# A transformer block on one core: u and the merge's gates as half-size block products, the merge's two products moved apart

## Chip, core and metric

The kernel runs on one core of one Trainium2 chip. The metric is the device time of one execution in microseconds (us); lower is better. The chip's engines are named as the profile names them: PE (TensorE matmul), PEld (its weight loads), DVE (VectorE), ACT (ScalarE), POOL (GpSimd) and SP (SyncE, which here only issues DMAs).

## The reference, cut to what matters

All data is float32; 512 tokens, width 1024. `h` is a layer norm of the input. Eight slices of one wide projection of `h` feed two branches, which are merged through sigmoid gates:

```
proj = h @ w_in + b_in
u, v, q, f, i, g, ga, gb = split(proj)
y_a = gelu(u) * (per group of 128 channels: masked w_s @ layer_norm(gelu(v)) + b_s)
y_b = hgrn2(q, f, i) rms-normed * silu(g)
merged = sigmoid(ga) * (y_a @ w_a) + sigmoid(gb) * (y_b @ w_b)
h1  = layer_norm(ALPHA * h + merged @ w_o)
out = layer_norm(ALPHA * h1 + ffn(h1) + ple(h1, p))
```

## The kernel before, in words

Every float32 product is made of three matmuls on rounded parts: each operand is split into a high part (a copy rounded by ACT, line 63) and a low part (the difference, on DVE, line 66). `hh`, `hl` are the parts of `h` transposed (channels on partitions, 512 tokens along a row), `ybh`, `ybl` those of y_b, `yah`, `yal` those of y_a, `mgh`, `mgl` those of `merged`.

`gemm_a` (line 85) makes 256 output channels for all 512 tokens. It loads two weight units of 512 KB, splits each, and runs 48 matmuls with 512 columns. `gemm_b` and `mm_b` (lines 98 to 121) make the products whose result has tokens on partitions. `strassen` (line 165) makes the product of two 2x2 block matrices with seven block products in place of eight: X, Z, Y, Z2, Y2, W, Y3. Each block product is 24 matmuls with 256 columns (`product_a`, line 218). It needs sums of weight blocks: POOL adds t1 and t2 (line 185), and two more are accumulated by DMAs issued on POOL's queue (line 183). Its activation operands are blocks of the activations and sums of such blocks (`combine`, line 134). In the kernel before, only the feed-forward stage (`up`, line 897) uses it, eleven times; its weight tiles are in the pool `wx` (line 800) except for the first block and t1, which are in `wpool`.

The order of stages is: start, recurrence (f, q, g projections of four head pairs), v (line 699), then the part that the change touches:

- u by four `gemm_a` calls (`proj`, line 750), with `norm_v` (layer norm of v, line 711), `finish` of the last head pair (line 644, which gives the last part of y_b) and `mix` (line 732: the spatial product of v, then times gelu(u), then the split into `yah`, `yal`) in between;
- the merge (lines 781 to 795): four rounds of ga, w_a, gb, w_b, each a `gemm_a`, with the gates' sigmoid on ACT, two multiplies and an add on DVE, and the split into `mgh`, `mgl`; each round also calls `residual` (line 774), which loads a slice of x again and scales it on ACT and POOL into `r1`;
- w_o (line 809 on), first norm `norm1`, transposes `turn`, the gate of the embedding branch, then the feed-forward stage.

The order on each engine is set by the framework's scheduler: it walks the program by priority, which is program order, and issues on each engine the first instruction that its own timing model has as ready. So an independent later product can be pulled into a gap. On the chip each engine then runs its instructions in that fixed order and waits on semaphores. Tiles are taken from pools that are stacked on the left and on the right side of the on-chip memory; a pool opened after others were closed lies where those lay, and its tiles wait until the closed pools' tiles have been read for the last time. `wpool` has three buffers for raw weights and five for each split part; PSUM has four tiles of two banks.

Of the kernel before, what the change touches and what calls it, by code (L numbers as in the profile page):

```python
# [8 lines left out]
F32 = mybir.dt.float32  # L9
# [5 lines left out]
P = 128  # L15
D = 1024
# [17 lines left out]
def block_kernel(  # L34
# [50 lines left out]
    def gemm_a(ps, w, c0, acth, actl, name):  # L85

        for kh in range(2):
            h, l = unit_a(w, 4 * kh, c0, f"{name}_{kh}")
            for j in range(2):
                cs = slice(j * P, (j + 1) * P)  # L90
                for k in range(4):
                    kk = 4 * kh + k
                    first, last = kk == 0, kk == KT - 1
                    PE.matmul(ps[:, j, :], h[:, k, cs], acth[:, kk, :], start=first, stop=False)  # L94
                    PE.matmul(ps[:, j, :], h[:, k, cs], actl[:, kk, :], start=False, stop=False)  # L95
                    PE.matmul(ps[:, j, :], l[:, k, cs], acth[:, kk, :], start=False, stop=last)  # L96
# [602 lines left out]
    for c in range(2):  # L699
# [5 lines left out]
        for a in range(2):  # L705
# [15 lines left out]
    norm_v(3)  # L721
    hgb_cm.__exit__(None, None, None)

    rpool = ctx.enter_context(tc.tile_pool(name="rpool", bufs=1, side="right"))
    r1 = rpool.tile([P, TT, D], F32, name="r1")
    yapool_cm = tc.tile_pool(name="yapool", bufs=1, side="right")
    yapool = yapool_cm.__enter__()
    yah = yapool.tile([P, NH, T], F32R, name="yah")
    yal = yapool.tile([P, NH, T], F32R, name="yal")
    with tc.tile_pool(name="gm", bufs=1, side="right") as gp:  # L730
        bs = load_bc(gp, gm_b_s[0].rearrange("g t -> (g t)"), "bs")
        def mix(m, ug):
# [15 lines left out]
        prev = None  # L748
        for m in range(NH // 2):
            psu = proj(OU, m, "gu") if m else psu0  # L750
            ug = gp.tile([P, 2, T], F32, tag="ug", name=f"ug{m}", bufs=2)
            for a in range(2):
                S.activation(ug[:, a, :], psu[:, a, :], AF.Gelu_apprx_tanh, bias=bcol(OU, 2 * m + a))
            if m:
                mix(m - 1, prev)
            prev = ug
        mix(NH // 2 - 1, prev)
    gmv_cm.__exit__(None, None, None)


    mgpool_cm = tc.tile_pool(name="mgpool", bufs=1, side="right")
    mgpool = mgpool_cm.__enter__()
    mgh = mgpool.tile([P, KT, T], F32R, name="mgh")
    mgl = mgpool.tile([P, KT, T], F32R, name="mgl")
    with tc.tile_pool(name="mg", bufs=1) as mp:

        g0a = load_bc(mp, ln0_g, "g0a")
        b0a = load_bc(mp, ln0_b, "b0a")
        S.activation(g0a, g0a, AF.Copy, scale=ALPHA)
        S.activation(b0a, b0a, AF.Copy, scale=ALPHA)  # L770
        nmr = mp.tile([P, TT, 1], F32, name="nmr")
        V.scalar_tensor_tensor(out=nmr, in0=mr0[:, :, 0:1], scalar=-1.0, in1=mr0[:, :, 1:2], op0=ALU.mult, op1=ALU.mult)

        def residual(t):
            r = r1[:, t, :]
            nc.sync.dma_start(r, xv[:, t, :])
            S.activation(r, r, AF.Identity, scale=mr0[:, t, 1:2], bias=nmr[:, t, :])
            G.tensor_tensor(out=r, in0=r, in1=g0a, op=ALU.mult)
            G.tensor_tensor(out=r, in0=r, in1=b0a, op=ALU.add)

        for m in range(KT // 2):
            residual(m)
            res = []
            for nm, off, w, ah, al in (("a", OGA, wa, yah, yal), ("b", OGB, wb, ybh, ybl)):
                psg = ps_tile(f"ps_mg{nm}{m}")
                gemm_a(psg, win, off + 256 * m, hh, hl, f"g{nm}{m}")
                sg = mp.tile([P, 2, T], F32, tag="sg", name=f"sg{nm}{m}", bufs=3)
                for a in range(2):
                    S.activation(sg[:, a, :], psg[:, a, :], AF.Sigmoid, bias=bcol(off, 2 * m + a))
                psw = ps_tile(f"ps_mw{nm}{m}")  # L790
                gemm_a(psw, w, 256 * m, ah, al, f"w{nm}{m}")
                V.tensor_tensor(out=sg, in0=psw, in1=sg, op=ALU.mult)
                res.append(sg)
            V.tensor_tensor(out=res[0], in0=res[0], in1=res[1], op=ALU.add)
            split(mgh[:, 2 * m:2 * m + 2, :], mgl[:, 2 * m:2 * m + 2, :], res[0])
# [240 lines left out]
```

## Time and profile before

| what | value |
| --- | --- |
| median of 3 runs | 958.17 us (957.72 to 958.33) |
| the profiled execution's own time | 958.66 us |
| its span, first to last instruction | 956.9 us |
| PE busy | 936.7 us, 98% of the span |
| DVE, ACT, POOL busy | 592.0, 356.5, 218.2 us |
| mean granted clock of PE | 0.994 |

The profiled execution's time is its span and 1.8 us around it. PE's busy time is modelled (matmuls overlap in the pipeline), so the cost of a matmul is read from the distance of two starts, not from its length.

### The profile page before, as it was taken

Reading aid. Unit: us, or ns where it says so; the run is one execution under the profiler, and the core shown is the slowest. Engines: PE = TensorE matmul, PEld = TensorE weight load, DVE = VectorE, ACT = ScalarE, POOL = GpSimd, SP = SyncE. Lnnn points to the kernel's source line nnn. Section 1 sums busy time; section 2 is a strip of 40 time slices with the busy share of each in tenths; the row PEclk is TensorE's granted clock in tenths of the full one; section 3 lists DMA queues with packets and bytes.
Section 4 is the critical chain, followed back from the end, with each engine's and each line's share of the span. In section 5 each row is a group of like instructions: output and inputs, shape, how many; then the busy total and the mean of one; then the engine's idle time right before and its main releaser. Section 6 shows DMA issues by size and latency. Waiting matters only on the chain.

```text
span 956.9 us, 13354 instructions
## 1 busy us (share of the span) xinstructions
PE 936.7 (98%) x5545; PEld 811.5 (85%) x5545; DVE 592.0 (62%) x652; ACT 356.5 (37%) x424; POOL 218.2 (23%) x148
## 2 busy tenths in 40 slices
PE   6999999999999999999999999999999999999996
PEld 5788888878888888888888887899999999988885
DVE  6748753948348756323243278588878888557517
ACT  3343232332333463222232267454435445333211
POOL 6415230315005218000000000534433340000004
PEclk8999999999999999999999999999999999999999
DMA  7542223221522633322324313965676664258302
GB/s 255 176 143 89 68 66 110 67 78 57 174 88 67 204 104 110 104 94 88 110 88 156 126 50 99 248 181 133 168 165 176 154 153 113 77 189 269 124 25 88
DMA packets 85452, 120.46 MB, mean 126 GB/s; under 512 B 3992, under 2 KB 60944, under 8 KB 85392
## 3 DMA queue, kind: packets, MB, share of 16 engines
q1 hardware_dynamic: 80880, 105.92, 34.6%
q0 software_dynamic: 3168, 11.54, 7.1%
q10 hardware_dynamic: 1344, 2.16, 0.6%
q8 instruction: 43, 0.70, 0.3%
q14 instruction: 17, 0.14, 0.1%
HBM read 101.77 MB, written 6.29 MB: 113 GB/s over the span
## 4 chain that ended last, share of the span: by engine, by line
PE 87%; DVE 7%; ACT 2%; POOL 2%; issue 1%; DMA 1%; DVEq 0%; ACTq 0%; POOLq 0%
PE ps_f_b L226 4%; PE ps_f_b L228 4%; PE ps_f_b L229 4%; PE ps_d L102 4%; PE ps_d L100 4%; PE ps_d L101 4%; PE ps_f_a L226 3%; PE ps_f_a L229 3%; PE ps_f_a L228 3%; PE ps_mwa L95 2%; PE ps_mwa L96 2%; PE ps_mwa L94 2%; PE ps_i L102 2%; PE ps_f L94 2%; PE ps_v L100 2%; PE ps_mgb L95 2%
## 5 line engine op out<-in xcount | busy, mean ns | idle before, releaser
L253 POOL TENSOR_TENSOR mr<-mr,nhalf 128x1 f32<-128x1 f32 x12 | 8.2, 684 | 323.4 <-DVE mr L252 323.4
L63 ACT CAST wh_f<-raw_f 128x1024 fp32r<-128x1024 f32 x41 | 43.1, 1051 | 87.4 <-PE ps_f_b L228 38.4
L102 PE MATMUL ps_d<-wh_d,hidl 128*128 128x512 f32 x172 | 66.8, 389 | 0.0
L101 PE MATMUL ps_d<-wl_d,hidh 128*128 128x512 f32 x172 | 66.8, 389 | 0.0
L66 DVE TENSOR_TENSOR wl_f<-raw_f,wh_f 128x1024 fp32r<-128x1024 f32 x41 | 52.8, 1289 | 21.4 <-ACT wh_f L63 21.3
L100 PE MATMUL ps_d<-wh_d,hidh 128*128 128x512 f32 x172 | 66.0, 389 | 0.0
L66 DVE TENSOR_TENSOR wl_f_t<-t_f,wh_f_t 128x1024 fp32r<-128x1024 f32 x22 | 55.4, 2519 | 3.0 <-ACT wh_f_t L63 2.7
L185 POOL TENSOR_TENSOR t_f<-raw_f,raw_f 128x1024 f32<-128x1024 f32 x11 | 26.7, 2428 | 126.5 <-DVE wl_f L66 102.7
L63 ACT CAST wh_d<-raw_d 128x1024 fp32r<-128x1024 f32 x22 | 23.1, 1050 | 62.1 <-PE ps_d L102 23.3
L482 POOL TENSOR_TENSOR k<-sgm,lv 128x512 f32<-128x512 f32 x8 | 15.8, 1994 | 121.9 <-DVE lv L534 121.9
L66 DVE TENSOR_TENSOR wl_d<-raw_d,wh_d 128x1024 fp32r<-128x1024 f32 x22 | 26.9, 1223 | 18.8 <-ACT wh_d L63 18.8
L102 PEld LDWEIGHTS ps_d<-wh_d,hidl 128*128 128x128 f32 x172 | 32.3, 188 | 6.7
L101 PEld LDWEIGHTS ps_d<-wl_d,hidh 128*128 128x128 f32 x172 | 32.3, 188 | 6.6
L100 PEld LDWEIGHTS ps_d<-wh_d,hidh 128*128 128x128 f32 x172 | 32.2, 188 | 6.5
L63 ACT CAST wh_f_t<-t_f 128x1024 fp32r<-128x1024 f32 x22 | 23.2, 1053 | 32.5 <-PE ps_f_b L229 18.3
L185 POOL TENSOR_TENSOR t_f<-t_f,raw_f 128x1024 f32<-128x1024 f32 x11 | 35.1, 3189 | 0.9
L66 DVE TENSOR_TENSOR wl_wb<-raw_wb,wh_wb 128x1024 fp32r<-128x1024 f32 x8 | 14.2, 1778 | 25.7 <-ACT wh_wb L63 25.7
L66 DVE TENSOR_TENSOR wl_wa<-raw_wa,wh_wa 128x1024 fp32r<-128x1024 f32 x8 | 9.8, 1225 | 28.0 <-ACT wh_wa L63 28.0
L66 DVE TENSOR_TENSOR wl_wo<-raw_wo,wh_wo 128x1024 fp32r<-128x1024 f32 x8 | 9.8, 1223 | 25.8 <-ACT wh_wo L63 25.8
L102 PE MATMUL ps_i<-wh_i,hl 128*128 128x512 f32 x64 | 25.1, 391 | 0.4 <-DVE hl L66 0.4
L921 DVE TENSOR_TENSOR g<-p,ps_f_b 128x512 f32<-128x512 f32 x11 | 7.6, 688 | 28.8 <-PE ps_f_b L229 28.7
L94 PE MATMUL ps_q<-hh,wh_q 128*128 128x512 f32 x64 | 25.2, 394 | 0.0
(373 smaller groups left out, 3199.8 us busy)
## 6 DMA issues: line engine op xcount, KB each, us to landing
raw_f<-in_w_ffn_up_dram SPq DMA_DIRECT2D x22, 512.0 KB, 7.2
raw_f<-in_w_ffn_gate_dram SPq DMA_DIRECT2D x22, 512.0 KB, 3.8
raw_d<-in_w_ffn_down_dram SPq DMA_DIRECT2D x22, 512.0 KB, 3.6
raw_f<-raw_f POOLq DMA_DIRECT2D x11, 512.0 KB, 4.7
t_f<-raw_f POOLq DMA_DIRECT2D x11, 512.0 KB, 7.2
raw_i<-in_w_in_dram SPq DMA_DIRECT2D x8, 512.0 KB, 3.9
raw_f<-in_w_in_dram SPq DMA_DIRECT2D x8, 512.0 KB, 3.7
raw_q<-in_w_in_dram SPq DMA_DIRECT2D x8, 512.0 KB, 3.7
```

The costliest lines, as they stand in the source:

```text
L63: S.copy(h, src)
L66: (eng or V).tensor_tensor(out=l, in0=src, in1=h.bitcast(F32), op=ALU.subtract)
L94: PE.matmul(ps[:, j, :], h[:, k, cs], acth[:, kk, :], start=first, stop=False)
L95: PE.matmul(ps[:, j, :], h[:, k, cs], actl[:, kk, :], start=False, stop=False)
L96: PE.matmul(ps[:, j, :], l[:, k, cs], acth[:, kk, :], start=False, stop=last)
L100: PE.matmul(ps, acth[:, kk, ts], h[:, k, :], start=first, stop=False)
L101: PE.matmul(ps, acth[:, kk, ts], l[:, k, :], start=False, stop=False)
L102: PE.matmul(ps, actl[:, kk, ts], h[:, k, :], start=False, stop=last)
L185: G.tensor_tensor(out=d, in0=a, in1=b, op=ALU.add)
L226: PE.matmul(o, h[:, k, cs], ah[:, k, :], start=first and j == 0 and k == 0, stop=False, skip_group_check=True)
L228: PE.matmul(o, h[:, k, cs], al[:, k, :], start=False, stop=False, skip_group_check=True)
L229: PE.matmul(o, l[:, k, cs], ah[:, k, :], start=False, stop=last and j == 1 and k == 3, skip_group_check=True)
```

## The change

w_b's product runs right behind v, with its result kept in `mgf`. Meanwhile `combine_h` makes the sums of blocks of `h` that the block products need (POOL adds the parts up again, DVE subtracts, ACT and DVE split), and `mix` writes its result into `yaf` without u. u is then made by two calls of `group_a` (the body of `up`, made general), 512 channels each, and the gates by four calls, 256 channels of ga and of gb each. gelu(u) multiplies `yaf`; sigmoid(gb) multiplies `mgf`; sigmoid(ga) goes out to device memory and is loaded again for w_a's product, which comes last. `r1` takes the buffer of `mgf` and is formed during w_o. Pools: the weight tiles of the new groups (`wxh`) and their temporaries (`gt`) are opened on the left after `gmv` and `ybpool` are closed, so `wxh` lies where `ybh` and `ybl` lay; half of y_a's parts and the reloaded gate (`mg`) lie where `hh` and `hl` lay; the split of `merged` (now `mgs`, in a pool opened on the left during w_o) lies in part where the first half of y_a's parts lay.

```diff
     def gemm_a(ps, w, c0, acth, actl, name):
+        gemm_t(ps, w, c0, lambda kk: (acth[:, kk, :], actl[:, kk, :]), name)
+
+    def gemm_t(ps, w, c0, act, name):
...
-    def norm_v(t):
+    finish(M)
+    for t in range(TT):
         mr = gv.tile([P, 2], F32, tag="mrv", name=f"mrv{t}", bufs=2)
-        ln_stats(gv, [vn[:, t, 0:512], vn[:, t, 512:1024]], mr, f"v{t}")
+        ln_stats(gvv, [vn[:, t, 0:512], vn[:, t, 512:1024]], mr, f"v{t}")
         normed(vn[:, t, :], mr, gmg, gmb, True)
-
-    norm_v(0)
-    psu0 = proj(OU, 0, "gu")
-    norm_v(1)
-    finish(M)
-    norm_v(2)
-    norm_v(3)
...
+        def combine_h(i):
+            f = {}
+            for n, ks, t0 in (("21", 0, HT), ("22", 4, HT), ("11", 0, 0), ("12", 4, 0)):
+                at = (slice(None), slice(ks, ks + 4), slice(t0 + i * P, t0 + i * P + P))
+                f[n] = gp.tile([P, 4, P], F32, tag=f"f{n}", name=f"f{n}_{i}")
+                G.tensor_tensor(out=f[n], in0=hh[at].bitcast(F32), in1=hl[at].bitcast(F32), op=ALU.add)
+            f["s1"] = gp.tile([P, 4, P], F32, tag="fs1", name=f"fs1_{i}")
+            lo = slice(i * P, i * P + P)
+            for n, o, x, y in (("s1", "s1", "21", "22"), ("a7", "21", "21", "11"), ("a6", "11", "11", "s1"), ("a3", "12", "12", "11")):
+                V.tensor_tensor(out=f[o], in0=f[x], in1=f[y], op=ALU.subtract)
+                split(hcomb[n][0][:, :, lo], hcomb[n][1][:, :, lo], f[o])
...
-            V.tensor_tensor(out=mx, in0=mx, in1=ug, op=ALU.mult)
-            split(yah[:, 2 * m:2 * m + 2, :], yal[:, 2 * m:2 * m + 2, :], mx)
...
+        for m in range(KT // 2):
+            psw = ps_tile(f"ps_mwb{m}")
+            gemm_a(psw, wb, 256 * m, ybh, ybl, f"wb{m}")
+            S.copy(mgf[:, 2 * m:2 * m + 2, :], psw)
+            if m == 0:
+                combine_h(0)
+            elif m == 1:
+                mix(0)
+                mix(1)
+                combine_h(1)
+            elif m == 2:
+                mix(2)
+                mix(3)
     gmv_cm.__exit__(None, None, None)
+    ybpool_cm.__exit__(None, None, None)
...
+    def group_a(wx, fp, srcs, comb, name, out):
...
+        strassen(wx, [[src_a(w, 4 * a, c0) for w, c0 in srcs] for a in range(2)], name,
+                 "X Z Y Z2 Y2 W Y3", prod, evac)
...
+    with tc.tile_pool(name="wxh", bufs=1) as wx, tc.tile_pool(name="gt", bufs=1) as fp:
+        def out_u(q):
+            def out(i, j, o):
+                for a in range(2):
+                    S.activation(o[:, a, :], o[:, a, :], AF.Gelu_apprx_tanh, bias=bcol(OU, 4 * q + 2 * j + a))
+                y = yaf[:, 4 * q + 2 * j:4 * q + 2 * j + 2, HT * i:HT * i + HT]
+                V.tensor_tensor(out=y, in0=y, in1=o, op=ALU.mult)
...
+                if j == 0:
+                    S.dma_start(ga_dram[:, 2 * m:2 * m + 2, HT * i:HT * i + HT], o)
+                else:
+                    y = mgf[:, 2 * m:2 * m + 2, HT * i:HT * i + HT]
+                    V.tensor_tensor(out=y, in0=y, in1=o, op=ALU.mult)
...
+        for q in range(2):
+            group_a(wx, fp, [(win, OU + 512 * q + 256 * c) for c in range(2)], hcomb, f"u{q}", out_u(q))
+        yas_pool = yas_cm.__enter__()
+        for m in range(KT // 2):
+            group_a(wx, fp, [(win, OGA + 256 * m), (win, OGB + 256 * m)], hcomb, f"g{m}", out_g(m))
+            if m == 0:
+                split_ya(yas_pool, 0)
+    hpool_cm.__exit__(None, None, None)
...
+        split_ya(mp, 1)
+        for m in range(KT // 2):
+            ga = mp.tile([P, 2, T], F32, tag="ga", name=f"ga{m}", bufs=2)
+            nc.sync.dma_start(ga, ga_dram[:, 2 * m:2 * m + 2, :])
+            psw = ps_tile(f"ps_mwa{m}")
+            gemm_t(psw, wa, 256 * m, lambda kk: tuple(z[:, kk % 4, :] for z in yas[kk // 4]), f"wa{m}")
+            V.tensor_tensor(out=ga, in0=psw, in1=ga, op=ALU.mult)
+            o = mgf[:, 2 * m:2 * m + 2, :]
+            V.tensor_tensor(out=o, in0=o, in1=ga, op=ALU.add)
...
-        for m in range(KT // 2):
-            residual(m)
-            res = []
-            for nm, off, w, ah, al in (("a", OGA, wa, yah, yal), ("b", OGB, wb, ybh, ybl)):
-                psg = ps_tile(f"ps_mg{nm}{m}")
-                gemm_a(psg, win, off + 256 * m, hh, hl, f"g{nm}{m}")
...
```

## Rows read from the trace of the kernel before

**Rows 1.** The page's first part: busy us and share of each engine.

```profile
PE 936.7 (98%) x5545; PEld 811.5 (85%) x5545; DVE 592.0 (62%) x652; ACT 356.5 (37%) x424; POOL 218.2 (23%) x148
```

**Rows 2.** Waits of PE, longest first: total us, times, longest us.

```profile
PE ps_vec L379 <- DMA vec<-in_ln_b_dram: 7.2, 1, 7.2
```

**Rows 3.** Stretches: busy us of PE, PEld, DVE, ACT, POOL; clock; DMA.

```profile
295.00:347.00 52.00, 52.00 (x268) 44.36 (x266) 38.47 (x42) 22.54 (x26) 16.88 (x8) 1.00 0.43 137
...
605.00:815.00 210.00, 209.99 (x1770) 207.96 (x1769) 168.69 (x158) 98.89 (x111) 73.30 (x41) 1.00 0.66 160
```

**Rows 4.** Timeline of PE at the merge's products: start us, us, instruction.

```profile
434.76 0.39 PE L94 MATMUL ps_mga<-hh,wh_ga 128*128 128x512 f32 x1
...
445.64 0.39 PE L94 MATMUL ps_mwa<-yah,wh_wa 128*128 128x512 f32 x1
...
456.84 0.39 PE L94 MATMUL ps_mgb<-hh,wh_gb 128*128 128x512 f32 x1
...
511.38 0.39 PE L96 MATMUL ps_mgb<-hh,wl_gb 128*128 128x512 f32 x1
...
522.48 0.39 PE L100 MATMUL ps_wo<-wh_wo,mgh 128*128 128x512 f32 x1
```

**Rows 5.** Timeline of PE in the feed-forward stage: first matmuls of block products.

```profile
645.27 0.28 PE L226 MATMUL ps_f_b<-ca7h,wh_f_t 128*128 128x256 f32 x1
...
667.56 0.28 PE L229 MATMUL ps_f_a<-c11h,wl_f 128*128 128x256 f32 x1
...
670.19 0.28 PE L226 MATMUL ps_f_b<-c12h,wh_f 128*128 128x256 f32 x1
...
673.07 0.29 PE L226 MATMUL ps_f_b<-ca6h,wh_f_t 128*128 128x256 f32 x1
...
676.15 0.28 PE L226 MATMUL ps_f_b<-c22h,wh_f_t 128*128 128x256 f32 x1
...
678.87 0.28 PE L229 MATMUL ps_f_a<-cs1h,wl_f_t 128*128 128x256 f32 x1
...
801.37 0.28 PE L226 MATMUL ps_f_b<-ca7h,wh_f_t 128*128 128x256 f32 x1
```

**Rows 6.** Timeline of SP: issue of the first loads into the pool wx.

```profile
511.80 0.92 SPq L174 DMA_DIRECT2D raw_f<-in_w_ffn_up_dram  x2
```

**Rows 7.** The page's DMA issues: count, KB each, us from issue to landing.

```profile
raw_f<-in_w_ffn_up_dram SPq DMA_DIRECT2D x22, 512.0 KB, 7.2
raw_f<-in_w_ffn_gate_dram SPq DMA_DIRECT2D x22, 512.0 KB, 3.8
```

**Rows 8.** The page's costliest groups: busy us, mean ns | idle before, releaser.

```profile
L63 ACT CAST wh_f<-raw_f 128x1024 fp32r<-128x1024 f32 x41 | 43.1, 1051 | 87.4 <-PE ps_f_b L228 38.4
...
L66 DVE TENSOR_TENSOR wl_f<-raw_f,wh_f 128x1024 fp32r<-128x1024 f32 x41 | 52.8, 1289 | 21.4 <-ACT wh_f L63 21.3
...
L66 DVE TENSOR_TENSOR wl_f_t<-t_f,wh_f_t 128x1024 fp32r<-128x1024 f32 x22 | 55.4, 2519 | 3.0 <-ACT wh_f_t L63 2.7
L185 POOL TENSOR_TENSOR t_f<-raw_f,raw_f 128x1024 f32<-128x1024 f32 x11 | 26.7, 2428 | 126.5 <-DVE wl_f L66 102.7
```

**Rows 9.** Stretches around PE's longest wait, columns as in rows 3.

```profile
8.00:10.00 2.00, 0.00 (x0) 0.00 (x0) 1.25 (x3) 0.00 (x0) 0.98 (x1) 1.00 1.01 397
...
14.00:16.00 2.00, 1.74 (x8) 1.74 (x9) 2.00 (x4) 0.39 (x1) 1.53 (x1) 0.50 0.99 368
16.00:18.00 2.00, 2.00 (x9) 1.68 (x8) 2.00 (x4) 1.05 (x1) 2.00 (x1) 0.69 0.49 111
```

**Rows 10.** Instructions on gt: duration ns min/median/max, first and last start.

```profile
L66 DVE TENSOR_TENSOR ybl<-gt,ybh x1: 3416/3416/3416, 314.9 to 314.9; 128x1024 fp32r<-128x1024 f32 x1
```

**Rows 11.** Groups of DVE by line, 605 to 815 us, columns as in rows 8.

```profile
L927 DVE TENSOR_TENSOR hid<-u,g 128x512 f32<-128x512 f32 x19 | 13.0, 684 | 0.7 <-ACT g L925 0.7
```

**Rows 12.** Instructions on r in the merge, columns as in rows 10.

```profile
L776 SPq DMA_DIRECT2D r<-in_x_dram x4: 426/481/1249, 318.8 to 321.1; - x4
...
L778 POOL TENSOR_TENSOR r<-r,g0a x4: 2456/3422/3442, 355.3 to 364.4; 128x1024 f32<-128x1024 f32 x4
...
DMA to landing us min/median/max: 6.6/7.3/8.0
```

More of the change, by code (lines that the diff above doesn't have):

```diff
@@ L93, in gemm_a @@
                     first, last = kk == 0, kk == KT - 1
[L94 to L96 removed]
+                    ah, al = act(kk)
+                    PE.matmul(ps[:, j, :], h[:, k, cs], ah, start=first, stop=False)
+                    PE.matmul(ps[:, j, :], h[:, k, cs], al, start=False, stop=False)
+                    PE.matmul(ps[:, j, :], l[:, k, cs], ah, start=False, stop=last)
     def mm_b(ps, t, acth, actl, kk, h, l, k, first, last):
@@ L746, in mix @@
-            split(yah[:, 2 * m:2 * m + 2, :], yal[:, 2 * m:2 * m + 2, :], mx)
[L748 to L757, printed above, removed]
@@ new lines, in block_kernel, with prod, new, evac @@
+    gmv_cm.__exit__(None, None, None)
+    ybpool_cm.__exit__(None, None, None)
+    def group_a(wx, fp, srcs, comb, name, out):
+        psa, psb = ps_tile(f"ps_{name}_a"), ps_tile(f"ps_{name}_b")
+        bank = {"X": psa[:, 0, :], "Z": psa[:, 1, :], "Y": psb[:, 0, :], "W": psb[:, 1, :]}
+        v = {n: b.rearrange("p (a c) -> p a c", c=HT) for n, b in bank.items()}
+        t = {}
+        def prod(chain, units, n, first, last):
+            product_a(bank[chain], units, comb[n], first, last)
+        def new(n, bufs=1):
+            t[n] = fp.tile([P, 2, HT], F32, tag=n, name=f"{n}_{name}", bufs=bufs)
+            return t[n]
+        def evac(n):
+            if n == "p1":
+                S.copy(new("p1", 2), v["X"])
+            elif n in ("y6", "z5"):
+                V.tensor_tensor(out=new(n), in0=v[n[0].upper()], in1=t["p1"], op=ALU.subtract)
+            else:
+                i, j = int(n[1]) - 1, int(n[2]) - 1
+                x, y, op = {"c11": (v["W"], "p1", ALU.add), "c22": (v["Y"], "z5", ALU.add),
+                            "c12": (v["Z"], "y6", ALU.add), "c21": (v["Y"], "p1", ALU.subtract)}[n]
+                o = new(f"{'gu'[j]}{i}")
+                if n == "c21":
+                    V.tensor_tensor(out=o, in0=t[y], in1=x, op=op)
+                else:
+                    V.tensor_tensor(out=o, in0=x, in1=t[y], op=op)
+                out(i, j, o)
+        strassen(wx, [[src_a(w, 4 * a, c0) for w, c0 in srcs] for a in range(2)], name,
+                 "X Z Y Z2 Y2 W Y3", prod, evac)
@@ L808, in block_kernel @@
         h1f = lp.tile([P, KT, T], F32, name="h1f")
+        mgpool_cm = tc.tile_pool(name="mgpool", bufs=1)
+        mgpool = mgpool_cm.__enter__()
+        mgs = [tuple(mgpool.tile([P, 2, T], F32R, name=f"mg{z}{m}") for z in "hl") for m in range(KT // 2)]
+        for m in range(KT // 2):
+            split(*mgs[m], mgf[:, 2 * m:2 * m + 2, :])
+        r1 = rpool.tile([P, TT, D], F32, tag="big", name="r1")
+        g0a = load_bc(mgpool, ln0_g, "g0a")
+        b0a = load_bc(mgpool, ln0_b, "b0a")
+        S.activation(g0a, g0a, AF.Copy, scale=ALPHA)
+        S.activation(b0a, b0a, AF.Copy, scale=ALPHA)
+        nmr = mgpool.tile([P, TT, 1], F32, name="nmr")
+        V.scalar_tensor_tensor(out=nmr, in0=mr0[:, :, 0:1], scalar=-1.0, in1=mr0[:, :, 1:2], op0=ALU.mult, op1=ALU.mult)
+        for t in range(TT):
+            r = r1[:, t, :]
+            nc.sync.dma_start(r, xv[:, t, :])
+            S.activation(r, r, AF.Identity, scale=mr0[:, t, 1:2], bias=nmr[:, t, :])
+            G.tensor_tensor(out=r, in0=r, in1=g0a, op=ALU.mult)
+            G.tensor_tensor(out=r, in0=r, in1=b0a, op=ALU.add)
         acc = [ps_tile(f"ps_wo{t}") for t in range(TT)]
```

113 lines of the change are left out of this document (44 added, 69 removed).

## The prediction

> **What bounds the kernel now.** I read the engines' shares first: PE is busy for 98% of the span and the next engine, DVE, for 62% [rows 1]. Then PE's waits: the longest is 7.2 us, in the first 15 us, and nothing in the stretch of the change comes near it [rows 2]. Then the stretches: from 295 to 347 us and in the feed-forward stage PE is busy all the time while DVE has 13.5 and 41 us free [rows 3]. Then the starts of single matmuls, since busy time overlaps. A product of 48 matmuls with 512 columns takes 10.88 us (ga) or 11.20 us (w_a) from its first start to the next product's first [rows 4], 227 or 233 ns a matmul. PE's own number of columns sets the time here, so a change is worth what it takes from PE, less the gaps that it opens.
>
> **The change, part by part.** A measurement of this kernel tells about 0.2%, 1.9 us, from no change. The sum is made against the profiled execution's 958.66 us, which is 0.49 us above the median.
>
> *Removed:* four products for u, four for ga, four for gb, each like ga's 10.88 us [rows 4]: 130.6 us.
>
> *Added:* six groups of seven block products. In the feed-forward stage the same block product (a7) begins at 645.27 and, eight groups later, at 801.37: 19.51 us a group [rows 5], 117.1 us for six. Difference **-13.5 us**. Bounds: a block product takes 2.72 us (22) to 2.88 us (12) [rows 5]; seven are 19.0 to 20.2, so -16.6 to -9.4. The mean stands, since the new groups have the same mix.
>
> *Moved:* w_b's and w_a's products, `mix`'s 64 matmuls, `finish`. Same matmuls, so zero; if the two rates of rows 4 go with the place of an operand, 1.3 us either way (192 matmuls at 6.6 ns).
>
> *Door 1, v to w_b.* `finish` now stands right before w_b. Behind its transposes come two multiplies (0.7 each, near rows 11), a copy (1.05) and a subtraction (1.29, at worst 3.42) [rows 8, 10]: 3.8 to 5.9 us. w_b's first 30 matmuls (6.8 us) need only earlier parts of y_b. Zero; at most 2 if v's own DVE work comes first.
>
> *w_b's stretch.* DVE loses eight full-width operations (multiply by u, y_a's low parts: 8 x 1.29 = 10.3) [rows 8] and gains `combine_h`'s sixteen half-width ones (16 x 0.69 = 11.0) [rows 11]: 38.5 becomes 39.2 in about 52 us [rows 3]. POOL gains eight half-width adds, about 1.2 each (half of 2.43) [rows 8], after the norm of v. These sums are wanted only at the first Z. 0.5 us; bounds 0 to 4.
>
> *Door 2, w_b to u.* This is the dear one. `wxh` lies where y_b's parts lay, so its loads wait for w_b's last matmul. The trace has the like: `wx` lies where `h`'s parts lay, the last matmul that reads them starts at 511.38 [rows 4], and the first load is issued at 511.80 [rows 6], far ahead of use, so it cost nothing. Here its use follows at once. X needs only the first block, which sits in `wpool`. Z needs t1: issue 0.4, load 3.8 (7.2 for the later of a pair) [rows 7], POOL add 2.43, copy 1.05, subtraction 2.52 beside POOL's next add or 1.29 without [rows 8]: 10.2 us, bounds 9.0 and 13.6. In it PE has X, 2.9 us, and can have the next group's X as well: in the feed-forward stage the next X (c11, 667.56) stands ahead of the present group's W (c12, 670.19) [rows 5]. I take both: 10.2 - 5.8 = 4.4 us of idle PE; bounds 3.2 and 10.7 (late load, one X). Then the clock. In PE's 7.2 us wait the granted clock was still 1.00 in the slice from 8 to 10 us, and 0.50 (1.2 for 2.4 GHz) when work came back at 14.26; up to 18 us that lost 1.74 x 0.50 + 2.0 x 0.31 = 1.5 us [rows 2, 9]. I add it whole: **+5.9**, bounds 3.2 (clock kept) and 12.2.
>
> The Trainium skill (TensorE: Matmul & The Clock Gate, Why this matters for your kernels) says to leave no idle gaps between bursts of matmuls, since the clock halves; rows 9 agree, at a gap longer than mine.
>
> *The six groups' other engines.* DVE has 168.7 / 210 x 19.51 = 15.7 us a group [rows 3]; u's groups have two half-width multiplies more (17.0), and a split of y_a (2 x 1.29) falls in the first gate group (18.3). ACT has 9.2 a group and gets six short activations more. Eight writes of the gate leave from ACT's queue. All below 19.51: zero, as long as DVE's order holds; the third rival is the case where it does not.
>
> *Door 3, gates to w_a.* The second half of y_a's split waits for the last product that reads `h`, then needs 1.05 + 1.29 for its first two slices and as much for the next. w_a's first half product (5.6 us) fills this, unless the scheduler has spent it on waits inside the last group: from a7's end (667.56) to 22's start (676.15) lie 8.6 us [rows 5], filled by other groups before, by w_a here. SP has the gate's reload (four loads) in its queue, waiting for the same release; a weight load behind it would be late by a load and a split, but `wpool` can hold the first units earlier. **+1.0**; bounds 0 and 5.
>
> *w_o with the residual.* `r1` takes `mgf`'s buffer, so x is loaded after the last split of `merged`: some 5 us into w_o (two DVE passes, a copy, a subtraction, rows 8), landing 7 later, then ACT, then eight POOL passes of about 3.2 [rows 12], 25 us in all, done near 38 us; the first slice is ready at 20 if each slice gets its add at once, at 29 if the four multiplies go first. PE reaches the first norm after 120 matmuls, 27.5 us, and the fourth at 44. What waits on POOL behind these passes is the norm's square root. **+0.5**; bounds 0 and 4.
>
> Sum: -13.5 + 0.5 + 5.9 + 1.0 + 0.5 = -5.6; 958.66 - 5.6 = 953.1, and against the median **952.6 us**.
>
> **Rivals.**
> 1. *Door 2 closes.* If the scheduler finds other ready work, or only part of y_b must have been read, PE stays busy and only the other 2.0 us are paid: 958.2 - 13.5 + 2.0 = 946.7 us. For it: the scheduler filled every gap of the feed-forward stage. Against: I find no third product that needs neither the pool nor the sums.
> 2. *Door 2 costs all, and more* (slower). PE's order is fixed, and if W or Y stands early in it, each of the first block products waits for its own part: the third load of a row (rows 7 give 7.2 for a second), t2 after t1 (another POOL add and a split at 2.52), t3 after a DMA on POOL's queue. An idle time of 10.7, 1.5 of clock and about 3 for the next waits is 15.2; the total is -13.5 + 15.2 + 2.0, so 962 us. It decides from 13.4 us on at that door. For it: nothing can be loaded ahead. Against: loads overlap, and one late X fills 2.9.
> 3. *DVE becomes the bound.* In the feed-forward stage a subtraction takes 2.52 us when POOL adds beside it and 1.29 otherwise [rows 8]. If u's groups run at 17.0 of work plus the 3.8 us that DVE idles a group now for its inputs, 20.8, that is 2.6 us more for two groups; w_b's stretch slips by up to 1: 952.6 + 3.6 = 956.2 us, at the edge of what can be told from no change.
>
> The Trainium skill (SBUF — State Buffer, Who interferes with whom) has a rule that speaks against this change: a DVE instruction with two inputs in SBUF and a POOL instruction that reads SBUF exclude each other for a whole instruction. Rows 8 agree in kind; by that rule `combine_h`'s adds and the new groups' would give the third rival's time.
>
> **How the numbers follow.** The forecast has 0.56, with a range of its own of 949 to 956. Rival 1 has 0.13, rival 2 0.15, rival 3 0.12; 0.04 is for several small gaps that lift the forecast to no change. Faster by over 0.2% (below 956.3): 0.56 + 0.13 + 0.01 of the third = 0.70. Within: 0.15. Slower (above 960.1): 0.15. The range reaches down to rival 1 and up short of rival 2's time: 945 to 960.
>
> **What would show it.** In the new profile the six groups repeat at 19.5 us; w_b's last matmul is followed by one or two X products, then by an idle PE of 3 to 11 us ended by DVE's low part of t1, and a slice with a clock below 1.00 behind it; the first loads of `wxh` are issued 0.4 us after that matmul. No wait of over 2 us stands at w_a or w_o. The prediction is wrong if the groups' period is above 20.2 us, if PE does not idle at that door, or if the residual's passes hold up the first norm.

## The result, and the profile after

The changed kernel takes **970.0 us** (969.1 to 970.7) where the kernel before takes 958.3: a ratio of 1.0122 (95% interval 1.0108 to 1.0136). It is slower by 11.8 us; the forecast was faster by 5.6. The profiled execution took 969.42 us, with a span of 967.7 against 956.9.

First the page's shares, the row that answers to [rows 1]:

```profile
PE 932.6 (96%) x5977; PEld 827.9 (86%) x5977; DVE 660.7 (68%) x730; ACT 391.8 (40%) x484; POOL 270.7 (28%) x180
```

PE's busy time did fall, from 936.7 to 932.6 us, although parts of it ran at half clock; the span grew, so PE idles more. PE's waits (total us, times, longest) say where; of these rows only the first was there before [rows 2]:

```profile
PE ps_vec L383 <- DMA vec<-in_ln_b_dram: 7.2, 1, 7.2
PE ps_u_a L230 <- ACT wh_u_t L63: 4.7, 1, 4.7
PE ps_u_b L230 <- DVE u_u L808: 3.7, 2, 2.7
PE ps_g_b L230 <- DVE u_g L808: 1.8, 1, 1.8
PE ps_u_a L233 <- DVE wl_u_t L66: 1.6, 1, 1.6
...
PE ps_pg L104 <- ACT c11h L63: 1.4, 1, 1.4
...
PE ps_h L925 <- ACT r L949: 1.3, 1, 1.3
PE ps_mx L756 <- POOL vn L275: 1.2, 1, 1.2
```

The first matmuls of the stages, from the timelines of PE, place the loss (us from the span's start; the last two columns are versions tried below):

| | before | after | door open | door open, adds on DVE |
|---|---|---|---|---|
| end of v | 295.4 | 295.4 | | |
| u's first X | | 348.43 | 348.16 | 348.96 |
| w_o | 522.48 | 529.69 | 515.96 | 513.38 |
| feed-forward | 614.64 | 625.03 | 608.17 | 605.51 |
| span | 956.9 | 967.7 | 950.3 | 946.7 |

So 7.2 us are lost up to w_o, 3.2 from w_o to the feed-forward stage (95.3 us for 92.2), 0.4 behind. The six groups should have won 13.5 in the first of these stretches: 13.5 + 10.8 = 24.3 us have to be found. Two places stand out in the timeline of the changed kernel (start us, us, engine, instruction; in brackets the idle time before it and its releaser):

```profile
348.43 0.28 PE L230 MATMUL ps_u_a<-hh,wh_u 128*128 128x256 f32 x1
348.62 6.04 SPq L178 DMA_DIRECT2D raw_u<-in_w_in_dram  x7
351.18 0.28 PE L233 MATMUL ps_u_a<-hh,wl_u 128*128 128x256 f32 x1
352.67 2.34 POOL L189 TENSOR_TENSOR t_u<-raw_u,raw_u 128x1024 f32<-128x1024 f32 x1 [14.08 <-DMA raw_u<-in_w_in_dram]
355.04 1.04 ACT L63 CAST wh_u_t<-t_u 128x1024 fp32r<-128x1024 f32 x1 [2.90 <-POOL t_u L189]
356.11 3.65 DVE L66 TENSOR_TENSOR wl_u_t<-t_u,wh_u_t 128x1024 fp32r<-128x1024 f32 x2 [10.80 <-ACT wh_u_t L63]
356.13 0.58 PE L230 MATMUL ps_u_a<-hs1h,wh_u_t 128*128 128x256 f32 x1 [4.67 <-ACT wh_u_t L63]
358.57 0.58 PE L233 MATMUL ps_u_a<-hs1h,wl_u_t 128*128 128x256 f32 x1 [1.64 <-DVE wl_u_t L66]
363.43 0.41 PE L230 MATMUL ps_u_b<-ha6h,wh_u_t 128*128 128x256 f32 x1
...
372.01 0.28 PE L230 MATMUL ps_u_a<-hh,wh_u 128*128 128x256 f32 x1
...
390.97 2.41 POOL L189 TENSOR_TENSOR t_g<-raw_g,raw_g 128x1024 f32<-128x1024 f32 x1 [10.46 <-DVE wl_g L66]
391.41 3.06 DVE L66 TENSOR_TENSOR yal<-yaf,yah 128x1024 fp32r<-128x1024 f32 x1
393.46 3.25 POOL L189 TENSOR_TENSOR t_g<-t_g,raw_g 128x1024 f32<-128x1024 f32 x1
394.39 3.40 DVE L66 TENSOR_TENSOR wl_g_t<-t_g,wh_g_t 128x1024 fp32r<-128x1024 f32 x1
397.72 0.68 DVE L831 TENSOR_TENSOR yaf<-yaf,u_u 128x512 f32<-128x512 f32 x1
398.32 0.68 DVE L808 TENSOR_TENSOR u_u<-ps_u_b,z_u 128x512 f32<-128x512 f32 x1
...
399.05 0.58 PE L230 MATMUL ps_u_b<-hh,wh_u 128*128 128x256 f32 x1 [2.71 <-DVE u_u L808]
404.13 0.41 PE L233 MATMUL ps_u_b<-hh,wl_u 128*128 128x256 f32 x1
```

**The door from w_b to u**, 348 to 366 us. The first loads go out 0.4 us after w_b's last matmul, as [rows 6] let expect. One X covers 2.9 us; Z's first matmul waits 4.7 us, its first with a low part another 1.6. The X of the next group stands at 372.01, not in the gap. **The waits for W**, at 376, 399 and 443 us: W's bank lies in the same PSUM tile as Y's, and its first matmul waits for DVE's pass over Y (c22, line 808). Each time that pass stands on DVE behind passes that POOL's adds stretch: at 399 behind two low parts of 3.06 and 3.40 us, at 376 behind one of 3.06, at 443 behind a low part of 2.93 and a multiply of 2.87. The stretches (columns as in [rows 3]) show the clock, and how far DVE had got:

```profile
345.00:390.00 45.00, 37.72 (x278) 36.24 (x277) 31.15 (x28) 20.65 (x27) 19.87 (x11) 0.89 0.86 234
390.00:435.00 45.00, 42.28 (x334) 41.70 (x333) 35.50 (x33) 23.92 (x34) 14.70 (x8) 0.92 0.56 136
...
356.00:358.00 2.00, 0.80 (x2) 0.50 (x2) 1.89 (x1) 0.62 (x2) 2.00 (x2) 0.50 1.09 352
...
400.00:402.00 2.00, 2.00 (x12) 2.00 (x11) 1.82 (x3) 1.36 (x2) 0.86 (x1) 0.50 0.83 130
```

At the granted clock of 0.50 (1.2 of 2.4 GHz) a matmul of 256 columns starts every 0.213 us, at 1.00 every 0.113 to 0.120. From 356.13 to Y's end at 366.57 PE needs 10.44 us for 48 matmuls, 1.64 of them the wait; at full clock they are 5.45, so the clock costs some 3.3 there. W at 399 takes 5.1 for 2.9: another 2.2.

**The account:** door 4.8 idle + 1.6 + 3.3 of clock = 9.7. Waits for W 1.0 + 2.7 + 1.8, and 2.2 of clock = 7.7. w_b's stretch 1.9 (348.43 - 295.37 = 53.1, for w_b's 192 matmuls, `mix`'s 64 and the transposes; these are 43.5, 6.9 and 0.8 by the distances of starts before), 1.2 of it the wait for `vn`. From w_o on 3.2. That is 22.5 of 24.3; 1.8 stay unnamed, 0.4 of them behind the feed-forward stage's first matmul.

### The profile page after: what moved, and what is told of

Read it like the earlier page. It is cut to its first block, busy times and chain, and to the rows that moved or that the text cites. A ratio compares the mean times of both kernels' runs of the same rounds, so it can differ in the third digit from the quotient of the medians.

```text
span 967.7 us, 14512 instructions
## 1 busy us (share of the span) xinstructions
PE 932.6 (96%) x5977; PEld 827.9 (86%) x5977; DVE 660.7 (68%) x730; ACT 391.8 (40%) x484; POOL 270.7 (28%) x180
## 3 DMA queue, kind: packets, MB, share of 16 engines
q0 software_dynamic: 4896, 17.83, 10.8%
## 4 chain that ended last, share of the span: by engine, by line
PE 80%; DVE 9%; POOL 3%; issue 3%; ACT 2%; DMA 2%; SPq 0%; DVEq 0%; POOLq 0%; ACTq 0%
PE ps_f_b L230 4%; PE ps_f_b L232 4%; PE ps_f_b L233 4%; PE ps_d L106 4%; PE ps_d L105 4%; PE ps_d L104 4%; PE ps_f_a L230 3%; PE ps_f_a L233 3%; PE ps_f_a L232 3%; PE ps_i L106 2%; PE ps_mwa L98 2%; PE ps_v L104 2%; PE ps_f L98 2%; PE ps_mwa L99 2%; PE ps_mwa L100 2%
## 5 line engine op out<-in xcount | busy, mean ns | idle before, releaser
L66 DVE TENSOR_TENSOR wl_f<-raw_f,wh_f 128x1024 fp32r<-128x1024 f32 x41 | 53.0, 1294 | 21.8 <-ACT wh_f L63 21.6
L63 ACT CAST wh_g<-raw_g 128x1024 fp32r<-128x1024 f32 x20 | 20.9, 1046 | 40.8 <-PE ps_g_b L232 10.8
L66 DVE TENSOR_TENSOR wl_g<-raw_g,wh_g 128x1024 fp32r<-128x1024 f32 x20 | 25.3, 1263 | 15.3 <-ACT wh_g L63 15.3
L896 POOL TENSOR_TENSOR r<-r,g0a 128x1024 f32<-128x1024 f32 x4 | 11.5, 2893 | 80.8 <-ACT r L895 80.8
L806 DVE TENSOR_TENSOR g_f<-p_f,ps_f_b 128x512 f32<-128x512 f32 x11 | 7.6, 687 | 28.8 <-PE ps_f_b L233 28.8
```

Source lines behind the costliest of these rows:

```text
L63: S.copy(h, src)
L66: (eng or V).tensor_tensor(out=l, in0=src, in1=h.bitcast(F32), op=ALU.subtract)
```

## The experiments

Each was timed beside the kernel before on the same chip, which took 958.6 to 958.7 us there; times are medians, differences are against the changed kernel's 970.0, measured on another occasion beside 958.3. The stretch from w_o to the feed-forward stage differs between the versions by up to 6 us for a reason of its own (told with w_o below), so in places the stretch from u's first X to w_o is given beside the time: 181.3 us in the changed kernel.

**The door open.** The six groups' pool of loads goes where `vn` lay, free at the end of `mix`, with six buffers for raw weights in place of eight; y_b stays, and y_a's halves take its place afterwards. The gate's reload takes the place of the row sums, the residual's two vectors get a pool of their own.

```diff
-                pool, bufs = (wpool, 3) if a + b == 0 else (wx, 8)
+                pool, bufs = (wpool, 3) if a + b == 0 else (wx, nb)
...
-    ybh = ybpool.tile([P, NH, T], F32R, name="ybh")
+    ybh = ybpool.tile([P, NH, T], F32R, tag="yb0", name="ybh")
...
-    ybpool_cm.__exit__(None, None, None)
...
-        h = pool.tile([P, 4, T], F32R, name=f"yah{k}")
-        l = pool.tile([P, 4, T], F32R, name=f"yal{k}")
+        hl2 = pool.tile([P, 2, 4, T], F32R, tag=f"yb{k}", name=f"ya{k}")
+        h, l = hl2[:, 0], hl2[:, 1]
...
-                split_ya(yas_pool, 0)
+                split_ya(ybpool, 0)
...
-            ga = mp.tile([P, 2, T], F32, tag="ga", name=f"ga{m}", bufs=2)
+            ga = hcpool.tile([P, 2, T], F32, tag=("hs1h", "hs1l", "ha6h", "ha6l")[m], name=f"ga{m}")
...
-        g0a = load_bc(mgpool, ln0_g, "g0a")
+        g0a = load_bc(rspool, ln0_g, "g0a")
```

> One part undone: the loads of the block products no longer wait for the last matmul that reads y_b. The six groups' pool of loads takes the place of vn and of the third norm's vectors, which come free at the end of mix; y_b's memory is reused for the halves of y_a, the gate's reload takes the place of the row sums, and the two vectors of the residual get a memory of their own (each tile of loads has 6 buffers for 8, and the residual's first vectors can come sooner). Theory (the door costs what the trace of the changed kernel shows there: 4.8 us of idle PE, a wait of 1.7, and some 3.2 of half clock, 9.7 in all): u's first Z follows its X without a gap, the granted clock stays at 1.00, and the time falls by 8 to 10 us, from 970.0 to about 961. Rival (the later waits at W would only grow by what the door gives back, since DVE is what the groups wait for): the gap at the door closes, but the time falls by less than 4 us.

Measured: 952.5 us, 17.5 less, and a ratio of 0.9937 to the kernel before (0.9924 to 0.9949). Both expectations were too low. In the stretch where the changed kernel's DVE had done 28 instructions and PE 278, they now did 39 and 351, at full clock:

```profile
345.00:390.00 45.00, 43.32 (x351) 41.97 (x350) 40.95 (x39) 26.07 (x36) 21.44 (x13) 1.00 0.79 188
```

**The two halves of that edit, alone.** `door_only` keeps the reload and the two vectors where the change put them; `reload_only` moves only these.

> The run with the door open made two changes of memory at once and came to 952.5 us, 17.5 below the changed kernel's 970.0. This is its first half alone: the six groups' loads lie where vn lay and y_a's halves where y_b lay, so no load waits for the last matmul of w_b; the gate's reload and the residual's two vectors stay where the changed kernel has them. Theory (the door costs its own 9.7 us and brings on the waits for DVE ahead of W too, some 4 more: with the door open the groups ended 13.1 us earlier): 970.0 - 13 to 14, about 956.5 us. Rival (the waits ahead of W went because the gate's reload and the residual's vectors no longer wait): the door's own 9.7 alone, about 960.

> The other half alone: the gate's reload lies where the row sums of h lay, and the residual's two vectors in a memory of their own; the door stays shut. Theory (in the output projection the door-open run won 3.1 us since the splits of the merged row and the loads behind them came sooner, the rest is the door's): 970.0 - 3, about 967 us. Rival (those 3 us came from the groups' earlier end, which moved the loads of the next weights): no change, 969 to 970.5.

Measured: 956.7 us (13.4 less) and 965.3 us (4.7 less); the sum, 18.1, is near the 17.5 that both gave together. The door is the larger part, and most of the waits for W go with this edit. In `door_only` they are 0.47 and 0.50 us:

```profile
387.72 0.39 PE L230 MATMUL ps_u_b<-hh,wh_u 128*128 128x256 f32 x1 [0.47 <-DVE u_u L807]
...
408.12 0.39 PE L230 MATMUL ps_g_b<-hh,wh_g 128*128 128x256 f32 x1 [0.50 <-DVE u_g L807]
...
518.02 0.77 PE L104 MATMUL ps_wo<-wh_wo,mgh 128*128 128x512 f32 x1 [4.71 <-issue]
```

The edit did two things to these waits, though. The loads come early, and POOL's two adds no longer run back to back: the second waits for a pass of DVE, so it stands 11 us behind the first and away from the passes in front of W.

```profile
382.96 2.41 POOL L189 TENSOR_TENSOR t_g<-raw_g,raw_g 128x1024 f32<-128x1024 f32 x1 [6.97 <-DVE wl_g L66]
...
394.05 2.77 POOL L189 TENSOR_TENSOR t_g<-t_g,raw_g 128x1024 f32<-128x1024 f32 x1 [4.04 <-DVE wl_g_t L66]
```

Every version with the door open has six buffers for eight, and where POOL adds its adds are apart like this from the second group on. No version has the door shut and the adds apart, so no run separates which of the two took the waits for W away.

The last PE row is a new door. From u's first X to the end of w_a `door_only` needs 164.7 us for the changed kernel's 181.3, 16.6 less; then w_o waits 4.7 us, since all four splits of `merged` begin behind the last product of w_a (ACT's first cast of them at 516.88 us), and starts at a granted clock of 0.50. With the reload moved as well that wait is gone. `reload_only` has the same wait for W at 399 us, without the loss of clock:

```profile
398.73 0.39 PE L230 MATMUL ps_u_b<-hh,wh_u 128*128 128x256 f32 x1 [2.70 <-DVE u_u L808]
...
401.58 0.28 PE L233 MATMUL ps_u_b<-hh,wl_u 128*128 128x256 f32 x1
```

From first to last matmul W takes 2.85 us here, 5.08 in the changed kernel. But the clock was lost at the next wait instead, a shorter one:

```profile
440.59 0.39 PE L230 MATMUL ps_g_b<-hh,wh_g 128*128 128x256 f32 x1 [2.05 <-DVE u_g L808]
...
444.79 0.41 PE L233 MATMUL ps_g_b<-hh,wl_g 128*128 128x256 f32 x1
```

```profile
442.00:444.00 2.00, 2.00 (x12) 2.00 (x11) 1.50 (x2) 0.90 (x2) 0.87 (x1) 0.50 1.00 186
```

That W takes 4.20 us, with a granted clock of 0.50 between 442 and 444 us. So in the profiled execution only 0.9 us are won from u's first X to w_o (180.4 for 181.3), and 2.6 behind w_o (92.7 to the feed-forward stage for 95.3), near the 3 of the theory.

**u as before, the gates alone as block products.**

```diff
-        for q in range(2):
-            group_a(wx, fp, [(win, OU + 512 * q + 256 * c) for c in range(2)], hcomb, f"u{q}", out_u(q))
+        for m in range(NH // 2):
+            psu = proj(OU, m, "gu")
...
```

> u is computed as before the change, as four products of 48 matmuls with 512 columns, and stands between w_b and the gates; only the gates are block products. u then needs nothing from the pool that waits, and its 43.5 us (four of 10.88) cover the loads. Theory (the door is all that was wrong with the groups): four groups for eight products win two thirds of the 13.5, 9.0 us; the door's 9.7 and the waits ahead of W (5.8 with the clock) go, and 4.5 of the gain is given up: 970.0 - 9.7 - 5.8 + 4.5 = 959 us. Rival (DVE holds W up wherever the first group stands, since the split of y_a and the first loads meet there): the waits ahead of W stay, about 965.

Measured: 958.9 us, as the theory had it, no different from the kernel before (0.9993 to 1.0011). A door costs nothing when work that needs nothing from behind it stands in it: u's 192 matmuls follow w_b's without a wait, 348.39 to 391.91 us. That the sum came out is in part luck. Up to w_o this version is 13.9 us ahead of the changed kernel (515.79 for 529.69; the theory's terms give 11.0) and 6.7 ahead of the kernel before, and it loses 2.9 more than the changed kernel behind w_o (98.2 us for 95.3).

Of the waits for W one is left:

```profile
429.44 0.39 PE L230 MATMUL ps_g_b<-hh,wh_g 128*128 128x256 f32 x1 [1.20 <-DVE u_g L808]
```

It is the second gate group's, as the one at 443 us in the changed kernel, and here too POOL's two adds run back to back (422.47 to 428.2 us) beside a low part of 2.23 and a multiply of 2.89 us in front of it. So this wait needs no shut door. The other two belonged to u's groups, which this version does not have.

**W in X's bank.**

```diff
-        bank = {"X": psa[:, 0, :], "Z": psa[:, 1, :], "Y": psb[:, 0, :], "W": psb[:, 1, :]}
+        bank = {"X": psa[:, 0, :], "Z": psa[:, 1, :], "Y": psb[:, 0, :], "W": psa[:, 0, :]}
```

> The block product W goes into the bank of X in place of the bank beside Y, in the six groups and in the feed-forward stage, which share the function. In the changed kernel W's first matmul waits for DVE's pass over Y (c22), which reads the same PSUM tile, though another bank of it. Theory (the gaps of 1.1, 3.1 and 1.9 us ahead of W come from this order and not from too much work on DVE): the three gaps and the half clock behind the second (about 2.2 us) go, and the time falls by 6 to 9 us. Rival (DVE has too much to do in the first groups, and PE will wait for it at the next product, Y3, or in the next group): the gaps only move, and the time falls by less than 2 us.

Measured: 965.5 us, 4.5 less, between the two. PE's waits in the groups behind the door:

```profile
PE ps_u_a L230 <- ACT p_u L797: 1.9, 1, 1.9
PE ps_u_a L230 <- DVE u_u L808: 1.7, 1, 1.7
PE ps_g_a L230 <- DVE u_g L808: 1.0, 2, 0.5
```

5.5 us became 4.6, partly at other products, and no clock was lost behind them: about half of the gain is the clock's 2.2 us. The shared tile only says where PE waits, not why DVE is late.

**The split of y_a out of W's way.** First it was moved in the source, to behind the third gate group; then its pool was made one that opens only behind the groups.

```diff
-            if m == 0:
+            if m == 2:
                 split_ya(yas_pool, 0)
```

```diff
-            if m == 0:
-                split_ya(yas_pool, 0)
...
     with tc.tile_pool(name="mg", bufs=1) as mp:
+        split_ya(mp, 0)
         split_ya(mp, 1)
```

> The split of y_a's first half stands behind the third gate group in place of the first; nothing needs it before w_a's first product. Theory (the longest wait for W, 2.7 us at 396 us, comes from this split: its low part and the next load's low part stand ahead of c22 on DVE): the gap at 396 us and the half clock behind it go, 5 us in all, and no new one comes. Rival (the wait comes from the start of the groups as a whole: DVE is behind from the door on, and any work would do): the gap gets smaller by at most 1 us, or moves to the group that takes the split, and the time stays within 2 us.

> In the run with the split later in the source, DVE's low part of it still stood at 391.5 us: the scheduler put it where it had been. Here both halves of y_a's split lie in the pool that opens only when the groups are done, so it cannot stand among them. Theory (the wait of 2.7 us for W at 396 to 399 us, and the half clock behind it, come from this low part of 3.06 us, behind which W's pass c22 stands): that wait falls below 1 us; w_a then waits for a cast and a low part behind the last group, 3 to 6 us; the time stays within 2 us of 970.0, with the loss moved from 399 us to w_a. Rival (other work of DVE takes its place in front of c22): the wait at 399 stays at 2 us or more, w_a waits as well, 972 to 976.

Measured: 970.4 and 973.1 us. The first run tells nothing of the split: the scheduler put its low part at 391.52 us, where it had been (391.41). In the second it is gone, and another pass stands stretched in its place, so W still waits 2.1 us and w_a waits 2.0 on top of it, as the rival had it:

```profile
391.98 3.05 DVE L66 TENSOR_TENSOR wl_g_t<-t_g,wh_g_t 128x1024 fp32r<-128x1024 f32 x1
394.95 2.86 DVE L830 TENSOR_TENSOR yaf<-yaf,u_u 128x512 f32<-128x512 f32 x1
397.73 0.68 DVE L808 TENSOR_TENSOR u_u<-ps_u_b,z_u 128x512 f32<-128x512 f32 x1
```

The multiply takes 0.68 us elsewhere [rows 11], 2.86 here; POOL adds from 391 to 397 us in this part of the group.

**The adds of the weight blocks on DVE**, for the six groups, with the door shut and with it open (there with W in X's bank, whose own run follows).

```diff
-                    G.tensor_tensor(out=d, in0=a, in1=b, op=ALU.add)
+                    (add or G).tensor_tensor(out=d, in0=a, in1=b, op=ALU.add)
```

> The adds that form t1 and t2 of the six groups' loads run on DVE in place of POOL (two a group, 1.2 us each there against 2.4 to 3.3 on POOL); the feed-forward stage keeps them on POOL. The door stays shut. Theory (DVE's passes with two inputs are stretched while POOL adds, 3.06 and 3.40 us for 1.22 in front of the pass that W waits for at 399 us): with no POOL add beside them the waits ahead of W fall to under 1.5 us in all from 5.5, and the chain at the door gets 1 us shorter: 970.0 - 5, about 965 us. Rival (DVE has too much to do in any case, and 2.4 us more a group makes the waits longer): 970 to 975.

> The same adds on DVE, with the door open and W in X's bank (951.4 us). There PE still waits 3.7 us in the groups (0.9, 1.6, 0.6, 0.6), two of them behind a low part of 3.4 us that stands beside a POOL add. Theory (the stretch beside POOL's adds is what is left): 949 to 950 us. Rival (DVE's added work takes it back): 951 to 954.

Measured: **962.5 us**, 7.5 less, and **947.8 us**. The same passes of DVE, door shut:

```profile
393.00 1.22 DVE L66 TENSOR_TENSOR wl_g_t<-t_g,wh_g_t 128x1024 fp32r<-128x1024 f32 x1
394.13 1.22 DVE L189 TENSOR_TENSOR t_g<-raw_g,raw_g 128x1024 f32<-128x1024 f32 x1
395.26 1.22 DVE L66 TENSOR_TENSOR yal<-yaf,yah 128x1024 fp32r<-128x1024 f32 x1
396.40 0.69 DVE L808 TENSOR_TENSOR u_u<-ps_u_b,z_u 128x512 f32<-128x512 f32 x1
```

Each low part is back at 1.22 us. The waits for W fall from 5.5 to 1.4 us (1.1 and 0.3), Z begins after a wait of 3.4 us for 4.7; waits of 1.0 us for Y's weights and 1.3 us for the pass over Y are new. All of these stand in u's two groups, none in the gates'. The clock took part: X, Z and Y take 14.7 us for 18.1, with less of it at 0.50, and no W is at half clock. From u's first X to w_o this version needs 171.7 us, 9.6 less; behind w_o it loses 2.3 more than the changed kernel. DVE's busy time between 345 and 480 us hardly changes (31.9 + 39.7 + 30.5 = 102.1 for 101.0), with twelve adds of 1.22 us more in it: what the added work costs, the lost stretch gives back. So the amount of work is not what PE waited for.

**W in X's bank, and three small edits, with the door open.** The small edits: the split of y_a behind the third gate group; also `mix(0)` and `mix(1)` behind w_b's third product; and `mix` so with the residual's two passes on DVE (`V` for `G` in lines 896 and 897; the split where the changed kernel has it).

```diff
-            if m == 0:
+            if m == 2:
                 split_ya(ybpool, 0)
```

```diff
-                mix(0)
-                mix(1)
                 combine_h(1)
             elif m == 2:
+                mix(0)
+                mix(1)
                 mix(2)
```

> The door open, and W in X's bank as well. With the door open PE still waits 0.9 us for W (0.4 and 0.5) and 3.3 us for other products of the first groups (0.9, 1.1 and 1.3, behind passes of ACT and DVE). Theory (the bank gives each W a product's time more before it needs Y's pass, in 17 groups): 951.5 us, 0.5 to 1.5 less than with the door open alone. Rival (Y3 then waits where W did, or X's pass, now needed before W, holds W): 952 to 954.

> The door open, W in X's bank, and the split of y_a's first half behind the third gate group. With the door open and W in X's bank the longest wait in the groups, 1.6 us, is for a pass of DVE that stands behind this split's low part (3.36 us where POOL adds beside it). Theory (what is left in front of PE is DVE's order in the first groups, so moving 2.5 us of DVE's work away from them shows now, though it showed nothing with the door shut): 950 us, 1 to 2 less than 951.4. Rival (the third gate group takes the same wait over): 951 to 952.

> As the run before it, and the first two slices of mix stand behind w_b's third product in place of the second. In every run so far PE waits 1.1 to 1.2 us inside w_b for the norm of v, which POOL finishes late. Theory: this wait goes, 1.1 us less than the run before it. Rival (the four slices come so late that vn, whose memory the loads of the groups now take, comes free later, and the door shuts again for a part): 1 to 5 us more than the run before it.

> The door open, W in X's bank, mix later as in the run before it, the split where the changed kernel has it, and the residual's multiply and add on DVE. With the door shut this last edit changed nothing, since the loads and splits of the next weights were late there as well. Theory (with the door open the first norm is no longer held by POOL, and PE waits only 0.5 us behind w_o): within 1 us of the run before it. Rival (POOL's passes still hold the norms up by 2 us or more behind w_o): 2 us less than it.

Measured: 951.4, 951.6, 958.2 and 961.7 us. The bank gives some 1.0 us, no more than the measurement can tell (0.9911 to 0.9936 for 0.9924 to 0.9949), and the split nothing, as its rival had it. The later `mix`, 6.6 us more, is a miss by a cause that neither side had: the wait for the norm of v goes, as the theory had it, but its matmuls now stand where no PSUM tile is free until ACT has copied w_b's product, and PE waits 6.3 us:

```profile
PE ps_mx L756 <- ACT mgf L767: 6.3, 1, 6.3
```

**The residual on DVE.**

```diff
-            G.tensor_tensor(out=r, in0=r, in1=g0a, op=ALU.mult)
-            G.tensor_tensor(out=r, in0=r, in1=b0a, op=ALU.add)
+            V.tensor_tensor(out=r, in0=r, in1=g0a, op=ALU.mult)
+            V.tensor_tensor(out=r, in0=r, in1=b0a, op=ALU.add)
```

> The residual's multiply and add in the output projection run on DVE in place of POOL; all else as in the changed kernel. Theory (the first norm's square root stands on POOL behind the residual's passes: DVE has its variance ready at 561.5 us, POOL runs it at 565.9): the norm starts some 4 us earlier and the time falls by 2.5 to 3.5 us. Rival (the eight passes hold up DVE's own work on the output projection as long, or PE's loss behind the output projection is from something else, the loads of the next stage say): the time stays within 1 us or gets longer.

Measured: 970.7 us; the theory falls. POOL's square root of the first norm ran at 562.6 us in place of 565.9, as it said, but PE then waited elsewhere:

```profile
PE ps_pg L104 <- issue: 2.7, 1, 2.7
PE ps_pg L106 <- DVE c11l L66: 1.5, 1, 1.5
```

With the door open this edit, the last of the four above, was a miss on both sides: 3.5 us more than its neighbour. It made the stretch behind w_o 95.2 us long, where the neighbour with POOL has 92.2 (523.64 to 615.80).

## Why the prediction was wrong

The forecast was 5.6 us faster, and the profiled executions came out 10.8 us slower: 16.4 us to explain. The largest miss is the term put at zero for the groups (7.7), then the door (3.8), w_o (2.7) and w_b's stretch (1.4); Door 3 was 1.0 too dear, and 1.8 are unnamed. The 7.7 alone would have turned the sign; without it the others together still leave the change 3.1 us slower. The prediction's own sign of being wrong, a period of the groups above 20.2 us, is there: a7 begins at 369.29 and, five groups later, at 477.45, 21.6 us a group.

**Its own rows held.** v to w_b (Door 1) costs nothing. A group of seven takes 19.5 us where nothing is late: with the door open a7 begins at 424.96 and 444.49 in the last two steady groups. Gates to w_a (Door 3) costs nothing either: w_a's halves and the last group's products alternate from 480 us on without a wait. That the residual would be ready at 38 us into w_o was right too (36.2).

**Door 2, +5.9, measured 9.7.** The chain was right to a tenth: 10.2 us from w_b's end to t1's low part, measured 348.43 to 358.57. What failed is the step "I take both": only one X stood in it, and the other stayed at 372.01. PE's order is written before the run; that it had pulled the next X ahead in a stage without a door [rows 5] was no ground for this one. The clock was also mis-sized, 1.5 for 3.3, since one execution behind another kind of gap was taken as the price [rows 9].

**"All below 19.51: zero, as long as DVE's order holds"**: this step failed for 7.7 us. It compared sums of busy time in a group with the time of a group. What PE waited for was one pass, c22, and in front of it POOL's two adds stretched DVE's passes: by 1.8 us at 376 (3.06 for 1.22), by 1.8 and 2.2 at 399, by 1.7 and 2.2 at 443, each time more than the wait (1.0, 2.7 and 1.8). With the adds off POOL the waits for W are 1.1 and 0.3, and none in the gates' groups; with the adds on POOL and u in the door the gates' wait of 1.2 stays. The door has a part in u's groups: they start with nothing loaded, DVE idles for 10.8 us and then has many passes due, and even with the adds on DVE waits of 1.0, 1.3, 1.1 and 0.3 us are left there. With the door open the waits for W are 0.5 and 0.5, but there the adds stand apart as well. How much of the adds' 7.5 us is the stretch itself, how much the clock and how much the new order that the scheduler made of it, no run separates.

The third rival had the mechanism, and [rows 8] its number, a low part of 2.52 us beside POOL and 1.29 without, but priced it as a sum of work, 3.6 us. The rule of the Trainium skill that was weighed there (SBUF — State Buffer, Who interferes with whom) is borne out: 3.06 to 3.40 us beside a POOL add, 1.22 without, and the low part of 3.40 ends 1.1 us after the POOL add that it stood beside. The second rival had the sign and, at 962, still 8 us too little; the point from which it was to decide, 13.4 us at the door, was not reached at the door alone (9.7), but is with the waits for W added (17.4).

**w_b's stretch, +0.5, measured 1.9**: POOL ends the norm of v late, and PE waits 1.2 us for it. **w_o with the residual, +0.5, measured 3.2.** The times of the residual's steps were right; the loss is not POOL's queue alone, as the residual on DVE showed. It goes with PE's order behind w_o. In eight traces two matmuls of the next product stand between two of the norm's sets of transposes, and the stretch from w_o to the feed-forward stage is 95.2 to 98.4 us; in the eight others, the kernel before among them, it is thirteen, and 92.1 to 92.7 us (94.5 in `door_only`, whose w_o starts at half clock). The place of the reload and of the two vectors changes that order (2.6 us); why it does was not isolated.

**The first rival** (the door closes, 946.7) was almost the best version's time, 947.8: a gain of 10.5 us where it had 11.5. The nearness is not the rival's own mechanism alone: opening the door came to 952.5, and the rest took W in X's bank and the groups' adds on DVE.

## What to carry to other kernels

Ahead of a stage that reads from a reused pool, ask what releases the pool, and put work there that needs nothing from behind it; one that must wait costs its chain, then the clock (here 4.8 and 1.6 us of waiting, then 3.3). Look where POOL's passes fall beside DVE's passes with two inputs, above all in front of a pass that PE waits for. Whether an engine keeps up is read from the order of its queue in front of the pass that PE waits for, with the passes' durations beside their neighbour, and not from its share of a period. And moving a call in the source may move nothing: look in the trace where the instruction went.

The version to keep from here is the one with the door open, W in X's bank and the groups' adds on DVE: 947.8 us, a ratio to the kernel before of 0.9887 (0.9872 to 0.9902). Its waits of PE from w_b to the feed-forward stage:

```profile
PE ps_u_a L230 <- ACT p_u L796: 1.3, 2, 0.9
PE ps_mx L756 <- POOL vn L275: 1.2, 1, 1.2
PE ps_pg L106 <- DVE c11l L66: 0.5, 1, 0.5
PE ps_g_a L230 <- ACT p_g L796: 0.3, 1, 0.3
```

## What the hardware showed that was not expected

The same gap does not always cost the same clock: behind a wait of 2.71 us at 399 us W ran at 0.50 and took 5.08 us in the changed kernel; behind one of 2.70 us in `reload_only` it ran at 1.00 and took 2.85. In that same execution the clock fell to 0.50 behind a wait of 2.05 us, some 1 us after PE had begun again, and W took 4.20. The Trainium skill (TensorE: Matmul & The Clock Gate, Why this matters for your kernels) warns of idle gaps between bursts of matmuls; the rows agree that such a gap can halve the clock, and add that it need not.

A half-width multiply on DVE with both inputs in SBUF took 2.86 us beside a POOL add, four times its 0.68. It lost 2.2 us, as much as a full-width low part (3.40 for 1.22): what such a pass loses went with POOL's add beside it, not with its own size.
